# Delta-rule products issued back to back, two ticks ahead of a head's scores, nine idle matmuls for fourteen, and the norm's x loaded later

## The chip, the cores and the metric

One core of a Trainium2 chip. The metric is the device time of one execution in microseconds (us), the median of several runs.

## The reference

One layer with a mixer of three branches and an MLP, on 512 tokens of width 1024, in float32. `rms_norm` scales each token; `proj = h @ w_in` feeds all branches: the gated delta rule (4 heads of 128, in chunks; `step` is one of them), causal stick-breaking attention (8 heads of 64) and a short convolution.

```python
    h = rms_norm(x, norm_mix_pre[l])
    proj = h @ w_in[l]
...
    y_a = gdn_branch(gdn_qkv, gdn_gate, gdn_a, gdn_b, conv_qkv_w[l], gdn_a_log[l],
                     gdn_dt_bias[l], gdn_norm_w[l])
    y_b = stick_breaking_branch(sb_qkv)
    y_c = short_conv_branch(sc_x, sc_b, sc_c, conv_sc_w[l])
...
    merged = (gates[:, :, 0] * (y_a @ w_branch[l, 0]) + gates[:, :, 1] * (y_b @ w_branch[l, 1])
              + gates[:, :, 2] * (y_c @ w_branch[l, 2]))
    x = x + rms_norm(merged @ w_out[l], norm_mix_post[l])
    h = rms_norm(x, norm_ffn_pre[l])
    x = x + rms_norm(jnp.square(jax.nn.relu(h @ w_ff1[l])) @ w_ff2[l], norm_ffn_post[l])

...
def step(state, inp):
    q_c, k_c, u_c, w_c, a_c, gl_c = inp
    v_new = u_c - jnp.einsum("bhcd,bhde->bhce", w_c, state)
    o_c = (jnp.einsum("bhcd,bhde->bhce", q_c, state)
           + jnp.einsum("bhcs,bhse->bhce", a_c, v_new))
    state = state * gl_c[..., None, None] + jnp.einsum("bhcd,bhce->bhde", k_c, v_new)
    return state, o_c
```

## The kernel before, in words

Everything is one program on one core. A float32 product is made of three matmuls on a high and a low part of each operand; a weight is split by a cast on ScalarE (L143) and a subtraction on VectorE (L144) into a tile `hl`, of which there are three buffers. Loads of weights are issued by SyncE, in the order of the program's priorities.

*The start.* L245 and L246 issue `WN` idle matmuls on zeros (`warm`). Then, for each of eight blocks k of the width, xT (`xk`) and the value weights (`raw`) are loaded, x is scaled and split into `xh` and `xl` (L263, L264), and four banks `psv` take the value product, 96 matmuls. The table `XT` says at which k the pieces of `xtok` (x by tokens) are loaded; their squares (ScalarE, L270) are summed to the norm's factor: POOL makes `rstd`, VectorE the diagonal `dg`, PE the matmul `rb` that spreads it over the partitions, ScalarE copies it (L297). With `rb`, VectorE scales `xk` (L301), which is split into `hh` and `hl`; `vv` is the scaled value product, half of it by ScalarE (L308) and half by VectorE (L309). The first two projections (`conv` with NX = 2) use `xh`, `xl` and are scaled afterwards (`cv`, L419), the later ones use `hh`, `hl`. `decay()` sums `psab` over 16 matmuls on `hh` and `hl`, copies it (`abT`, L349), and turns it by four small matmuls into `psa`.

*The middle.* The projections (`proj`, 24 matmuls each) are PE's steady work. The branches are generators in four lanes. `proj` calls `tick()` after k = 2, 5 and 7, so a tick is nine or six matmuls of a projection; at a tick each lane runs its live generator on if the count of its last `yield` is used up. The order of the work is so written out by hand: by the yields' counts (`SBY`, `CY` and others) and by the table `YD`, which adds to single yields. Within it, a scheduler orders each engine's instructions by priority and data.

- `sb_head(h)`: the scores `z` (8 matmuls), then ScalarE and VectorE make the weights (Abs, Exp, Ln, Relu, a scan, a difference, a last Exp), and, `SBY[0]` = 7 ticks later with the offsets of `YD`, ten transposes `at`, which are split into `ah` and `al`. The lane has width 1, so the next head's scores follow when the generator ends. `sb_out` multiplies by `vv` into `pav`, `SBY[1]` ticks later.
- `gdn_chain(h)`: for each of four chunks the products pc, p2, p3, p4 and p5, `CY` ticks apart. Into the bank p5 go the state's product (`ktok`, left half) and the output's product (`AQ`, right half). Tiles that differ in a number alone are shown as one name in the profile, so p2 to p5 all read `p`; `ct` is the chain's scratch. `pa`, `PM`, `pb` and `T64` belong to the inverse before it (`gdn_inverse`).

Later come the branch products, the output projection and the MLP, up to 903 us; nothing of the change lies there.

Of the kernel before, what the change touches and what calls it, by code (L numbers as in the profile page):

```python
# [18 lines left out]
NB = T // P  # L19
# [16 lines left out]
    "mats2": {0: 11, 1: 3},  # L36
    "pair0": {0: 2},
    "pair2": {0: -2, 5: 1, 28: -2, 30: -1},
    "sb0": {0: 3},
    "sb1": {0: 4},  # L40
    "sb2": {0: 3},
    "sb3": {0: 4},
    "sb5": {0: 2},
    "sb6": {0: 1},
    "sb7": {0: 6},
}
SBY = (7, 10)
NX = 2
PFM = 2
WN = 14  # L50
IY = (2, 8, 4)
HY = (3, 3, 1)
CY = (4, 1)
DY = (3, 3)
MY = (1,)
GY = (1, 1, 4, 2, 1, 1, 1)
XT = ((), (), (0,), (1, 2), (3, 4), (5, 6), (7,), ())
VW_NM, VW_CQ, VW_CS, VW_NF, VW_GN = 0, 8, 56, 68, 76
VW = 77

# [2 lines left out]
def trunk_kernel(ctx, tc, keys, xT, xtok, wst, wab, cst, vec, alog, dtb, wpost, wffn, wfpost, out):  # L63
# [12 lines left out]
    def nm(s):  # L76
        cnt[0] += 1
        return f"{s}_{cnt[0]}"

    def g2(s, dt=F32, shape=(P, 512)):  # L80
        return gp.tile(list(shape), dt, tag="g2", name=nm(s))

    def bank(s="c"):
        return pp.tile([P, 512], F32, tag="c", bufs=5, name=nm(s))
# [93 lines left out]
    def mm(o, l, r, start=True, stop=True, more=False):  # L178
        return nc.tensor.matmul(o, l, r, start=start, stop=stop, skip_group_check=more)  # L179
# [6 lines left out]
    def split(hi, lo, src):  # L186
        nc.scalar.copy(hi, src)  # L187
        nc.vector.tensor_tensor(lo, src, rf(hi), ALU.subtract)  # L188
# [56 lines left out]
    pw = bank("warm")  # L245
    for _ in range(WN):  # L246
        mm(pw, wr[:, 0:128], wr)
# [6 lines left out]
    for k in range(KT):  # L254
        with early():
# [9 lines left out]
            split(wv[k][:, 0, :], wv[k][:, 1, :], raw)  # L265
            for j in XT[k]:
                b, hf = j // 2, j % 2
# [140 lines left out]
    qk, vT, gT, ktok, vs, AD, M1, M2, AQ, sqs, wD, ya = ({} for _ in range(12))  # L408
# [142 lines left out]
    def gdn_chain(h):  # L551
        S = None
        ot = vs[h]
        so = sm.tile([P, NB], F32, name=nm("so"))

        Sh = g2("S", F32, (P, NB, P))
        for n in range(NB):
            ct = g2("ct", F32, (P, 4, P))
            bs = slice(n * P, n * P + P)
            oq = None  # L560
            if n == 0:
                R = vs[h][:, 0, :]
            else:
                pc = bank("pc")
                mm(pc[:, 0:128], qk[h][0][:, bs], S)
                mm(pc[:, 128:256], qk[h][1][:, bs], S)
                R = ct[:, 0, :]
                nc.vector.scalar_tensor_tensor(R, pc[:, 0:128], neG[:, n, h:h + 1], vs[h][:, n, :],
                                               ALU.mult, ALU.add)
                oq = ct[:, 1, :]  # L570
                nc.scalar.mul(oq, pc[:, 128:256], eG[:, n, h:h + 1])
                yield CY[h // 2]
            p2 = bank("p2")
            mm(p2[:, 0:128], T64[h][:, n, :], R)
            z0 = ct[:, 2, :]
            nc.vector.tensor_copy(z0, p2[:, 0:128])
            yield CY[h // 2]
            p3 = bank("p3")
            mm(p3[:, 0:128], M2[h][:, n, :], z0)
            Y = ct[:, 3, :]  # L580
            nc.vector.tensor_copy(Y, p3[:, 0:128])
            yield CY[h // 2]
            p4 = bank("p4")
            mm(p4[:, 0:128], T64[h][:, n, :], Y)
            z = ct[:, 2, :]
            nc.vector.tensor_tensor(z, z0, p4[:, 0:128], ALU.subtract)
            if n < NB - 1:
                Xc = ct[:, 0, :]
                nc.vector.tensor_scalar(Xc, z, wD[h][:, n:n + 1], None, ALU.mult)
            yield CY[h // 2]  # L590
            p5 = bank("p5")
            if n < NB - 1:
                mm(p5[:, 0:128], ktok[h][:, n, :], Xc)
                Sn = Sh[:, n, :]
                if n == 0:
                    nc.vector.tensor_copy(Sn, p5[:, 0:128])
                else:
                    nc.vector.scalar_tensor_tensor(Sn, S, gl[:, n, h:h + 1], p5[:, 0:128], ALU.mult, ALU.add)
                S = Sn
            mm(p5[:, 128:256], AQ[h][:, n, :], z)  # L600
            if n == 0:
                nc.vector.tensor_copy(ot[:, n, :], p5[:, 128:256])
            else:
                nc.vector.tensor_tensor(ot[:, n, :], oq, p5[:, 128:256], ALU.add)
            jk = ct[:, 3, :]
            nc.scalar.activation(jk, ot[:, n, :], AF.Square, accum_out=so[:, n:n + 1])
            yield CY[h // 2]
        f = sm.tile([P, NB], F32, tag="f", bufs=2, name=nm("f"))
        c1 = EPS * P * P
        nc.vector.tensor_scalar(f, sqs[h][:, 1, :], c1, c1 * EPS, ALU.mult, ALU.add)  # L610
        nc.vector.tensor_tensor(f, f, so, ALU.add)
        nc.gpsimd.tensor_tensor(f, f, half[:, 0:1].to_broadcast([P, NB]), ALU.pow)
        nc.vector.tensor_tensor(ot, ot, f.unsqueeze(2).to_broadcast([P, NB, P]), ALU.mult)
        yield GY[6]
        po = bank("po")
        for n in range(NB):
            nc.tensor.transpose(po[:, n * P:n * P + P], ot[:, n, :], ident)
        y = g2("y")
        nc.vector.tensor_tensor(y, gT[h], po, ALU.mult)
        ya[h] = (g2("ya", F32R), g2("ya", F32R))  # L620
        split(ya[h][0], ya[h][1], y)
# [38 lines left out]
    def sb_head(h):  # L660
        pz = [bank("z") for _ in range(3)]
        for j in range(3):
            for b, c0 in SEG[j]:
                n, bs = 128 * b + 128, slice(b * P, b * P + P)
                mm(pz[j][:, c0:c0 + n], Qh[h][:, bs], Kt[h][:, :n], True, False)
                mm(pz[j][:, c0:c0 + n], Ql[h][:, bs], Kt[h][:, :n], False, True)
        w, z, c = ([g2(s) for _ in range(3)] for s in ("w", "z", "c"))

        for j in range(3):
            nc.scalar.copy(z[j][:, :N[j]], pz[j][:, :N[j]])  # L670
            c0, m = DIAG[j]
            keep_before(z[j][:, c0:c0 + 128 * m], m)
        for j in range(3):
            n = N[j]
            nc.scalar.activation(w[j][:, :n], z[j][:, :n], AF.Abs)
            (act(w[j][:, :n], w[j][:, :n], AF.Exp, scale=-1.0))
            (act(w[j][:, :n], w[j][:, :n], AF.Ln, bias=1.0))
            nc.scalar.activation(c[j][:, :n], z[j][:, :n], AF.Relu)
            for b, c0 in SEG[j]:
                ks = slice(c0, c0 + 128 * b + 128)  # L680
                back = c[j][:, ks][:, ::-1]
                nc.vector.tensor_tensor_scan(back, back, w[j][:, ks][:, ::-1], 0.0, ALU.add, ALU.add)  # L682
            nc.vector.tensor_tensor(z[j][:, :n], z[j][:, :n], c[j][:, :n], ALU.subtract)  # L683
            (act(z[j][:, :n], z[j][:, :n], AF.Exp))
        yield SBY[0]
        pt = [bank("at") for _ in range(3)]
        K0 = (((0, 0),), ((1, 0), (3, 384)), ((2, 0),))
        where = {b: (j, c0) for j in range(3) for b, c0 in SEG[j]}
        a = {}
        for j in range(3):  # L690
            for sb, c0 in K0[j]:
                for b in range(sb, NB):
                    o = c0 + (b - sb) * P
                    i, q0 = where[b]
                    nc.tensor.transpose(pt[j][:, o:o + P], z[i][:, q0 + sb * P:q0 + sb * P + P], ident)
            n = N[j]
            hi, lo = g2("ah", F32R), g2("al", F32R)
            split(hi[:, :n], lo[:, :n], pt[j][:, :n])
            for sb, c0 in K0[j]:
                m = 512 - sb * P  # L700
                a[sb] = (hi[:, c0:c0 + m], lo[:, c0:c0 + m])
        avl.add(f"av{h}", sb_out(h, a))

    def sb_out(h, a):
        i, e = h // 2, h % 2
        vv = [VV[b, h // 4][:, h % 4].rearrange("p j c -> p (j c)") for b in range(NB)]
        yield SBY[1]
        pav = bank("pav")
        for j in range(2):
            for sb in range(NB):  # L710
                mm(pav[:, sb * P:], vv[sb], a[sb][j], j == 0 and sb == 0, j == 1 and sb == NB - 1)
        if e == 0:
            y32[i] = g2("y32")
        tl = g2("tl")
        nc.scalar.copy(tl[0:64, :], pav[64:128, :])
        nc.vector.tensor_tensor(y32[i][64 * e:64 * e + 64, :], pav[0:64, :], tl[0:64, :], ALU.add)
        if e == 1:
            yb[i] = (g2("yb", F32R), g2("yb", F32R))
            split(yb[i][0], yb[i][1], y32[i])
# [399 lines left out]
    for tb in product(S, lambda u: W[u], lambda u: (S1[u], block(1, 0)(u)), False, 2):  # L1119
# [8 lines left out]
        z, c0 = tb  # L1128
# [97 lines left out]
```

## Time and profile before

| | us |
|---|---|
| median of 3 runs | 904.35 (902.25, 904.35, 904.47) |
| the profiled execution | 905.1 |
| its span | 903.4 |
| mean granted TensorE clock | 0.996 |

The profile is of one execution: the span runs from its first to its last instruction, and the device time beside it is 1.7 us longer. A row of the timeline has an instruction's start, its duration, and in brackets how long its engine sat idle before it and what ended that.

### The profile page before, as it was taken

To read this page: it belongs to the slowest core of one execution; us is meant where nothing else is said; L and a number is where in the kernel's file an instruction comes from. 1 tells how busy PE (TensorE), PEld (TensorE's weight loads), DVE (VectorE), ACT (ScalarE), POOL (GpSimd) and SP (SyncE) were. 2 spreads that over 40 slices of the span, in tenths; PEclk is the share of its full clock that TensorE was granted. 3 is DMA by queue.
4 is the path that set the end of the run, shared out by engine and by line. 5 is a ranking of instruction groups with operands and counts; after the bars stand their busy time and mean duration, and the time that the engine had idled before them with its cause. 6 is when DMAs were issued, how large, how long until landed. Compare 5 with 4: busy or idle time off the path is not lost.

```text
span 903.4 us, 11761 instructions
## 1 busy us (share of the span) xinstructions
PE 885.4 (98%) x4224; PEld 736.7 (82%) x4224; DVE 589.0 (65%) x1026; ACT 452.1 (50%) x825; POOL 105.8 (12%) x165
## 2 busy tenths in 40 slices
PE   9999999999999999999999999999999999999996
PEld 7788888877788888888888878988888888888885
DVE  4885678987777659655565546533334459878886
ACT  6556875657787732233344333322223237566562
POOL 1003221010112120200000111011111000000120
PEclk9999999999999999999999999999999999999998
DMA  9322223222113144524243552299999339566692
GB/s 313 125 86 82 70 79 118 73 103 71 68 38 106 50 127 121 162 90 117 70 152 126 173 191 94 98 288 288 284 286 269 122 111 373 187 194 203 190 267 103
DMA packets 41626, 136.97 MB, mean 152 GB/s; under 512 B 5456, under 2 KB 5456, under 8 KB 41184
## 3 DMA queue, kind: packets, MB, share of 16 engines
q1 hardware_dynamic: 34032, 111.24, 35.2%
q0 software_dynamic: 7248, 24.68, 13.0%
q8 instruction: 33, 0.54, 0.2%
q10 hardware_dynamic: 288, 0.30, 0.1%
q14 instruction: 25, 0.20, 0.1%
HBM read 131.48 MB, written 29.88 MB: 179 GB/s over the span
## 4 chain that ended last, share of the span: by engine, by line
PE 83%; DVE 10%; issue 3%; ACT 3%; DMA 1%; POOL 0%; DVEq 0%; POOLq 0%; SPq 0%; ACTq 0%
PE mm L179 51%; PE Q L179 5%; PE R L179 5%; PE po L179 5%; PE S L179 5%; PE psv L179 2%; PE V L179 2%; DVE hl L144 2%; DVE c L682 2%; PE p L179 2%; DVE z L683 1%; DVE XX L513 1%; PE pg L179 1%; DVE XX L507 1%; PE warm L179 1%
## 5 line engine op out<-in xcount | busy, mean ns | idle before, releaser
L179 PE MATMUL mm<-hh,hl 128*128 128x512 f32 x928 | 306.0, 397 | 0.9 <-ACT ct L729 0.9
L143 ACT CAST hl<-raw 128x1024 fp32r<-128x1024 f32 x116 | 111.6, 962 | 217.7 <-PE mm L179 189.0
L144 DVE TENSOR_TENSOR hl<-raw,hl 128x1024 fp32r<-128x1024 f32 x116 | 129.9, 1120 | 138.1 <-ACT hl L143 137.8
L179 PEld LDWEIGHTS mm<-hh,hl 128*128 128x128 f32 x928 | 174.1, 188 | 35.7 <-ACT ct L729 1.3
L179 PE MATMUL mm<-hl,hl 128*128 128x512 f32 x464 | 181.1, 390 | 0.0
L179 PE MATMUL mm<-h2h,hl 128*128 128x512 f32 (+1 forms) x528 | 155.0, 377 | 0.4 <-ACT h2h L187 0.2
L179 PEld LDWEIGHTS mm<-h2h,hl 128*128 128x128 f32 x528 | 97.2, 188 | 18.8 <-ACT h2h L187 0.8
L179 PEld LDWEIGHTS mm<-hl,hl 128*128 128x128 f32 x464 | 87.5, 189 | 16.0
L179 PE MATMUL mm<-h2l,hl 128*128 128x512 f32 (+1 forms) x264 | 99.5, 377 | 0.1
L997 DVE TENSOR_TENSOR hl<-ch,hl 128x1024 fp32r<-128x1024 f32 x53 | 64.6, 1223 | 6.2 <-ACT hl L996 6.1
L179 PEld LDWEIGHTS mm<-h2l,hl 128*128 128x128 f32 x264 | 49.7, 188 | 9.4 <-DVE h2l L188 0.3
L996 ACT CAST hl<-ch 128x1024 fp32r<-128x1024 f32 x53 | 55.3, 1046 | 0.0
L179 PE MATMUL po<-wo,mg 128*128 128x512 f32 x192 | 45.2, 391 | 0.0
L179 PEld LDWEIGHTS po<-wo,mg 128*128 128x128 f32 x192 | 35.8, 188 | 7.9 <-ACT mg L187 0.3
L179 PE MATMUL Q<-hl,ahi 128*128 128x512 f32 x128 | 39.7, 391 | 0.0
L179 PE MATMUL R<-hl,ahi 128*128 128x512 f32 x128 | 39.4, 389 | 0.0
L168 POOL DMA_DIRECT2D S<-wst x24 | 20.0, 832 | 151.9 <-DMA S<-wst 115.4
L179 PE MATMUL S<-hl,ahi 128*128 128x512 f32 x120 | 37.0, 389 | 0.0
L682 DVE TENSOR_TENSOR_SCAN c<-c,w 128x512 f32<-128x512 f32 (+3 forms) x32 | 25.5, 815 | 15.1 <-ACT w L106 15.0
L187 ACT CAST ahi<-aT 128x512 fp32r<-128x512 f32 x32 | 19.8, 622 | 28.7 <-PE Q L179 12.1
L179 PEld LDWEIGHTS Q<-hl,ahi 128*128 128x128 f32 x128 | 24.0, 188 | 5.7 <-ACT hl L996 0.4
L947 DVE TENSOR_TENSOR aT<-r,mm 128x256 f32<-128x256 f32 x62 | 23.1, 413 | 7.7 <-ACT r L942 7.7
(297 smaller groups left out, 1448.7 us busy)
## 6 DMA issues: line engine op xcount, KB each, us to landing
raw<-wst SPq DMA_DIRECT2D x92, 512.0 KB, 3.3
ch<-S SPq DMA_DIRECT2D x32, 512.0 KB, 4.3
raw<-wst SPq DMA_DIRECT2D x48, 256.0 KB, 3.2
S<-wst POOLq DMA_DIRECT2D x24, 512.0 KB, 8.7
ch<-wst SPq DMA_DIRECT2D x21, 512.0 KB, 5.2
S<-wst SPq DMA_DIRECT2D x16, 512.0 KB, 8.6
S<-S SPq DMA_DIRECT2D x8, 512.0 KB, 8.7
ch<-wst POOLq DMA_DIRECT2D x8, 512.0 KB, 8.7
```

What stands on the lines that cost most here:

```text
L143: nc.scalar.copy(hl[:, 0, :], raw)
L144: nc.vector.tensor_tensor(hl[:, 1, :], raw, rf(hl[:, 0, :]), ALU.subtract)
L168: nc.gpsimd.dma_start(t, wsrc(1024, *key), accum_op=ALU.add, max_dma_last_dim=4096)
L179: return nc.tensor.matmul(o, l, r, start=start, stop=stop, skip_group_check=more)
L187: nc.scalar.copy(hi, src)
L507: nc.vector.tensor_tensor(tmp[:, :, :w], X[:, :, j].unsqueeze(2).to_broadcast([P, 8, w]), L[:, j, j + 1:].unsqueeze(1).to_broadcast([P, 8, ...
L513: nc.vector.tensor_tensor(X[:, :, j + 1:], X[:, :, j + 1:], tmp[:, :, :w], ALU.subtract)
L682: nc.vector.tensor_tensor_scan(back, back, w[j][:, ks][:, ::-1], 0.0, ALU.add, ALU.add)
L683: nc.vector.tensor_tensor(z[j][:, :n], z[j][:, :n], c[j][:, :n], ALU.subtract)
L947: x = nc.vector.tensor_tensor(aT[i][u][:, f % 2, :], r[:, c], ps[:, c], ALU.mult)
L996: after[0] = nc.scalar.copy(hl[0][:, c], r)
L997: after[1] = nc.vector.tensor_tensor(hl[1][:, c], r, rf(hl[0][:, c]), ALU.subtract)
```

## The change

`gdn_chain` issues the product on `AQ` directly behind the one on `ktok`, ahead of VectorE's read of the state. `sb_head` yields two ticks more (`SBY[2]`) behind its transposes, and the offsets of the heads in `YD` are smaller. `WN` goes from 14 to 9. `XT` loads all of xtok at k = 4 to 7.

```diff
-    "sb0": {0: 3},
-    "sb1": {0: 4},
-    "sb2": {0: 3},
-    "sb3": {0: 4},
-    "sb5": {0: 2},
-    "sb6": {0: 1},
-    "sb7": {0: 6},
+    "sb0": {0: 1},
+    "sb1": {0: 2},
+    "sb2": {0: 2},
+    "sb3": {0: 3},
+    "sb4": {0: -2},
+    "sb5": {0: 0},
+    "sb6": {0: -1},
+    "sb7": {0: 5, 1: -2},
 }
-SBY = (7, 10)
+SBY = (7, 10, 2)
-WN = 14
+WN = 9
-XT = ((), (), (0,), (1, 2), (3, 4), (5, 6), (7,), ())
+XT = ((), (), (), (), (0, 1), (2, 3), (4, 5), (6, 7))
@@ gdn_chain
             if n < NB - 1:
                 mm(p5[:, 0:128], ktok[h][:, n, :], Xc)
+            mm(p5[:, 128:256], AQ[h][:, n, :], z)
+            if n < NB - 1:
                 Sn = Sh[:, n, :]
                 if n == 0:
                     nc.vector.tensor_copy(Sn, p5[:, 0:128])
                 else:
                     nc.vector.scalar_tensor_tensor(Sn, S, gl[:, n, h:h + 1], p5[:, 0:128], ALU.mult, ALU.add)
                 S = Sn
-            mm(p5[:, 128:256], AQ[h][:, n, :], z)
@@ sb_head
         avl.add(f"av{h}", sb_out(h, a))
+        yield SBY[2]
```

On PE, where psab ends and psa is issued (`mm_523` of before and `mm_518` of the change are the third projection, 24 matmuls, `hl_519` and `hl_514` its weights). Before:

```order
L179 MATMUL psab_442<-hl,wabs 16x512
L179 MATMUL mm_487<-xh_140,hl_483 128x512
L179 MATMUL mm_523<-hh,hl_519 128x512
...
L179 MATMUL mm_523<-hl,hl_519 128x512
L179 MATMUL mm_523<-hh,hl_519 128x512
L179 MATMUL psa_587<-cs,abT_459 128x8 x4
```

and in the change:

```order
L180 MATMUL psab_437<-hl,wabs 16x512
L180 MATMUL mm_518<-hh,hl_514 128x512 x2
L180 MATMUL mm_518<-hl,hl_514 128x512
L180 MATMUL mm_518<-hh,hl_514 128x512 x2
L180 MATMUL mm_518<-hl,hl_514 128x512
L180 MATMUL mm_518<-hh,hl_514 128x512
L180 MATMUL psa_582<-cs,abT_454 128x8 x4
```

Between the last psab and psa stood 25 projection matmuls, and seven stand there now. The matmul rb has moved the other way: it followed the last of psv directly, and now 15 matmuls of the first projection stand ahead of it.

On ScalarE, at the same place of the program (`hl_624` and `hl_619` are the fifth projection's weights, `hl_660` and `hl_655` the sixth's). Before:

```order
L143 CAST hl_624<-raw_623 128x1024
L308 ACTIVATE vv_385<-psv_238,rstd 128x4x64
L308 ACTIVATE vv_388<-psv_239,rstd 128x4x64
L308 ACTIVATE vv_391<-psv_239,rstd 128x4x64
L308 ACTIVATE vv_394<-psv_240,rstd 128x4x64
L308 ACTIVATE vv_397<-psv_240,rstd 128x4x64
L349 COPY abT_459<-psab_442 16x512
L143 CAST hl_660<-raw_659 128x1024
```

and in the change:

```order
L309 ACTIVATE vv_380<-psv_233,rstd 128x4x64
L309 ACTIVATE vv_383<-psv_234,rstd 128x4x64
L144 CAST hl_655<-raw_654 128x1024
L309 ACTIVATE vv_386<-psv_234,rstd 128x4x64
L309 ACTIVATE vv_389<-psv_235,rstd 128x4x64
L309 ACTIVATE vv_392<-psv_235,rstd 128x4x64
L350 COPY abT_454<-psab_437 16x512
```

The sixth conversion, which stood behind abT, stands ahead of the last three vv and of abT.

On PE, at the last step of the first chunk of the heads 0 and 1 of the delta rule (`p_429` and `p_430` are their banks p5, `mm_2420` and `mm_2415` a projection, `at` the transposes of the sixth attention head). Before:

```order
L179 MATMUL p_429_2430<-ct_2158,ktok_869 128x128
L179 MATMUL p_430_2436<-ct_2164,ktok_1090 128x128
L179 MATMUL mm_2420<-hh,hl_2416 128x512
...
L179 MATMUL mm_2420<-hh,hl_2416 128x512
L179 MATMUL p_429_2430<-ct_2158,AQ_1020 128x128
L179 MATMUL p_430_2436<-ct_2164,AQ_1267 128x128
L695 MATMUL at_2457<-cs,z_2265 128x128
```

and in the change:

```order
L180 MATMUL p_429_2425<-ct_2153,ktok_864 128x128
L180 MATMUL p_429_2425<-ct_2153,AQ_1015 128x128
L180 MATMUL p_430_2431<-ct_2159,ktok_1110 128x128
L180 MATMUL p_430_2431<-ct_2159,AQ_1262 128x128
L180 MATMUL mm_2415<-hh,hl_2411 128x512
L180 MATMUL mm_2415<-hl,hl_2411 128x512
```

The AQ products stood 15 projection matmuls behind the ktok products, directly ahead of the transposes; now each stands behind its ktok product, and nine projection matmuls lie between them and the transposes.

## Rows read from the trace of the kernel before

**Rows 1.** The page, part 1: busy time, share of the span, instructions of each engine.
```profile
PE 885.4 (98%) x4224; PEld 736.7 (82%) x4224; DVE 589.0 (65%) x1026; ACT 452.1 (50%) x825; POOL 105.8 (12%) x165
```
**Rows 2.** Waits of PE: who waited, for whom; us in total, times, longest.
```profile
PE warm L179 <- DVE wr L244: 2.0, 1, 2.0
PE p L179 <- DVE S L596: 1.8, 1, 1.8
PE z L179 <- DVE al L188: 1.0, 1, 1.0
PE mm L179 <- ACT ct L729: 0.9, 1, 0.9
PE p L179 <- DVE ct L581: 0.8, 1, 0.8
...
PE z L179 <- DVE K L648: 0.7, 1, 0.7
PE pb L179 <- ACT PM L538: 0.5, 1, 0.5
PE p L179 <- DVE S L598: 0.3, 1, 0.3
...
PE p L179 <- DVE ct L568: 0.2, 1, 0.2
```
**Rows 3.** Windows: length, busy time of PE, PEld, DVE, ACT, POOL, PEclk, DMA share, GB/s.
```profile
250.20:253.55 3.35, 3.35 (x15) 3.16 (x14) 3.05 (x6) 2.05 (x8) 0.00 (x0) 0.50 0.19 45
...
176.00:178.00 2.00, 1.73 (x9) 1.48 (x10) 1.97 (x8) 2.00 (x6) 1.03 (x3) 1.00 0.00 0
```
**Rows 4.** Timeline of PE around the wait for S.
```profile
249.01 0.71 PE L179 MATMUL p<-ct,AQ 128*128 128x128 f32 x4 [1.83 <-DVE S L596]
249.56 1.72 PE L695 MATMUL at<-cs,z 128*128 128x128 f32 x10
```
**Rows 5.** Timeline of PE at the start: first idle matmul, first psv, rb.
```profile
1.98 6.19 PE L179 MATMUL warm<-wr 128*128 128x512 f32 x14 [1.98 <-DVE wr L244]
8.00 0.63 PE L179 MATMUL psv<-hl,xh 128*128 128x512 f32 x2
...
29.80 1.02 PE L179 MATMUL rb<-dg,cs 128*128 128x512 f32 x2
```
**Rows 6.** Timeline of ScalarE: the weights of the first two blocks.
```profile
4.92 0.60 ACT L187 CAST hl<-raw 128x512 fp32r<-128x512 f32 x1
...
9.10 0.62 ACT L187 CAST hl<-raw 128x512 fp32r<-128x512 f32 x1
```
**Rows 7.** Timeline of PE: last matmuls of the second and third projection, psa.
```profile
45.15 0.39 PE L179 MATMUL mm<-xh,hl 128*128 128x512 f32 x1
...
50.59 0.39 PE L179 MATMUL mm<-hh,hl 128*128 128x512 f32 x1
51.16 1.05 PE L179 MATMUL psa<-cs,abT 16*128 16x8 f32 x8 [0.17 <-ACT abT L349]
```
**Rows 8.** Timeline of ScalarE ahead of psa.
```profile
45.62 1.05 ACT L143 CAST hl<-raw 128x1024 fp32r<-128x1024 f32 x1 [1.47 <-issue]
46.58 0.83 ACT L308 ACTIVATE vv<-psv,rstd 128x256 fp32r<-128x256 f32 x2
...
50.54 0.56 ACT L349 COPY abT<-psab 16x512 f32<-16x512 f32 x1
```
**Rows 9.** Timeline of VectorE ahead of psa.
```profile
46.71 1.22 DVE L144 TENSOR_TENSOR hl<-raw,hl 128x1024 fp32r<-128x1024 f32 x1 [1.57 <-ACT hl L143]
47.85 0.87 DVE L309 SCALAR_TENSOR_TENSOR vv<-psv,rstd,vv 128x256 fp32r<-128x256 f32 x2
```
**Rows 10.** Timeline: first scores (PE) and last exp (ScalarE), fifth and eighth head.
```profile
206.10 0.47 PE L179 MATMUL z<-K,Qh 128*128 128x512 f32 x1 [0.73 <-DVE K L648]
...
217.88 0.42 ACT L106 ACTIVATE z<-z 128x256 f32<-128x256 f32 x1 [0.96 <-DVE z L683]
...
276.16 0.39 PE L179 MATMUL z<-K,Qh 128*128 128x512 f32 x1
...
287.72 0.42 ACT L106 ACTIVATE z<-z 128x256 f32<-128x256 f32 x1 [0.70 <-DVE z L683]
```

## The prediction

> **What bounds the kernel now.** I read the page's busy times first: TensorE's matmuls are busy for 98% of the span, VectorE for 65%, ScalarE for 50% [rows 1]. So only about 18 us exist in which PE does nothing, and the change leaves the number of useful matmuls as it is; whatever it wins or loses must be a PE wait, or a stretch in which PE's clock is low. The second view is therefore the list of PE's waits [rows 2]: 2.0 us before the first idle matmul, and eight short waits that belong to the branches that share the middle of the program: 1.8 on S, 1.0 on al, 0.9 on ct (L729), 0.8 on ct (L581), 0.7 on K, 0.5 on PM, 0.3 on S again and 0.2 on ct (L568), together 6.2 us, all of them between 176 and 289 us. The third is the windows view: after the longest of those waits the granted clock is 0.50 for 3.35 us, which is 1.2 GHz instead of 2.4; around the 1.0 us wait on al it stays at 1.00 [rows 3]. The fourth is the timeline at that place: the output products of the delta rule, `p<-ct,AQ`, sat 1.83 us behind VectorE's read of S [rows 4].
>
> **The start, idle matmuls.** Fourteen idle matmuls run from 1.98 to 8.00, 0.43 us apiece, and the 96 real ones after them take (29.80 - 8.00)/96 = 0.227 us apiece with no gap, up to the matmul rb [rows 5]. That is the low and the high level of the clock. With nine, the first real matmul can start at 1.98 + 9 x 0.43 = 5.85; its operands are there, since ScalarE's half of the first weights is done at 4.92 + 0.60 = 5.52 [rows 6]. PE has been at work for equally long at 8.0, so I let the clock rise there as before: five real matmuls run at 0.43 in place of five idle ones, and 5 x 0.227 = 1.13 us are won behind them. The other seven of the first input block end at 8.00 + 7 x 0.227 = 9.59; the second block's weights are ready at 9.10 + 0.62 = 9.72 [rows 6], a gap of 0.15. Term: **-1.0** (0 if the clock rises later by as much, -1.1 at best). Bringing xtok later gives these matmuls nothing by itself: they ran without a gap already.
>
> **The start, xtok.** What the later xtok does is to move its consumers. In the order of PE, rb stands 15 matmuls deeper, behind the value product rather than directly after it; its successors are pushed together, and psa, which had 25 projection matmuls between itself and the last psab, has seven. ScalarE's order changes with it: one more weight conversion (the one two behind hl_519, now called hl_655) stands ahead of three vv and of abT, where it used to stand behind abT. A conversion writes one of three weight buffers, and this one's is the buffer that the third projection reads until its last matmul. So ScalarE cannot pass before that projection ends, and psa, the very next thing on PE, needs abT from behind it. The same pattern one projection earlier gives the price: the last matmul of the second projection starts at 45.15 [rows 7], and then the conversion starts at 45.62 and ends near 46.58, the next two vv take 0.83 [rows 8], VectorE's half starts at 46.71 and is followed by two vv from 47.85, 0.87 long [rows 9]. Put in terms of the last matmul's start: conversion +0.47 to +1.43, two vv to +2.26, VectorE's half to +2.70, its two vv to +3.57, the last vv on ScalarE to +4.0, abT (0.56 [rows 8]) to +4.56, psa at **+4.6**. Before, psa started 51.16 - 50.59 = 0.57 behind the last matmul, 0.17 of it waiting [rows 7]. Term: **+4.0**, a PE wait of about 4.2 us that no row of before has. Least: +2.5, if ScalarE's vv do not wait for VectorE's; most: +5.0, if the conversion's own buffer is late too.
>
> **The clock after that wait.** No row shows a wait of 4.2 us inside the program. The nearest are the 1.83 us wait, after which 3.35 us ran at 0.50 and so lost 1.67 us [rows 3, 4], and the launch, where PE worked for 8.00 - 1.98 = 6.0 us at the low level, 3.0 us lost [rows 5]. The waits of up to 1.0 lost nothing [rows 2, 3]. I take the middle of the two losses, **+2.3**; 0 and +3.0 are the ends.
>
> **The middle, removed.** The two products of a step are issued back to back, so the output product no longer sits behind the read of S: that removes the 1.83 and the 0.3 [rows 2, 4]. The two ticks ahead of each next head's scores put 15 to 18 projection matmuls (3.4 to 4.1 us at 0.227) between the transposes and the scores, so the scores' wait for al, which is the copy of those transposes, goes, and so does that for K (0.7). The other four (0.9, 0.8, 0.5, 0.2) stand at places that the new offsets move as well, and in the new order their producers stand further ahead. I take all eight, 6.2 us, and the 1.67 us of low clock behind the longest: **-7.9**. The least is -4.6: the two on S, the one on al and the clock alone, with 0.2 to spare.
>
> What reads S now waits for two products rather than one. Two output products take 249.56 - 249.01 = 0.55 us [rows 4], so S comes 0.28 us later in each of twelve steps. In the order the next user of S stands six to nine matmuls away (1.4 to 2.0 us), so nothing of it shows; 12 x 0.28 = 3.3 us is the far end. Here the Trainium skill speaks against the change: PSUM — Partial Sum Buffer, section "PSUM bank collisions raise a hardware error", says that two engines are kept apart by bank and quadrant, and that another address in the same bank still collides. By that rule reading S must wait for the second product, as I have assumed, and the sum would be at most 3.3 us higher if nothing covered it; the trace agrees in so far as the output product, in the other half of the bank, waited 1.83 us for the read.
>
> **The middle, new waits.** The scores come later, the transposes mostly do not, so the chain from scores to transposes has less room. For the eighth head it takes 287.72 + 0.42 - 276.16 = 12.0 us from the first scores to the last exp, for the fifth 217.88 + 0.42 - 206.10 = 12.2 [rows 10]. In the new order the eighth head has 8 score matmuls (1.2 us), 21 of projections (4.8), 8 of pav (1.2), 9 small products (9 x 0.28 = 2.5) and 2 of psd (0.5) in between: 10.2 us, so its transposes wait about 1.7. The fifth head has 38 of projections (8.6), the scores (1.2), 8 products of pb (1.8) and 2 of p2 (0.6): 12.2, which is just enough; I take 0.5. A further 0.3 is for the output of the fifth head, whose copy stands close behind VectorE's other work. Term: **+2.5** (0 to +7).
>
> **The sum** is -1.0 + 4.0 + 2.3 - 7.9 + 2.5 = **-0.1 us**. The profiled execution took 905.1 us with a span of 903.4; the median of the three runs is 904.35. So I forecast **904.2 us**. About 0.3%, 2.7 us, is what a measurement of this kernel can tell from no change.
>
> **Rival 1, the waits simply go.** The wait at psa comes, but PE's clock does not fall behind it, and half of the new waits in the middle stay hidden: -1.0 + 4.0 - 7.9 + 1.2 = -3.7, 900.6 us. For it: the waits of up to 1.0 us left the clock at 1.00 [rows 3]. Against it: 1.83 us did not, and 4.2 is longer. If the wait at psa did not come either, it would be 896.6; the order speaks against that.
>
> **Rival 2, slower: the transposes wait.** In the middle the two ticks shift the waits from the scores to the transposes. If the fifth, sixth, seventh and eighth heads each wait 1.2 to 1.7 us there (the chain is 12 us or longer, and VectorE was busy for most of the stretch), that is 5.5 us in place of 2.5, and one of them is long enough to drop the clock again (1.67 [rows 3]): -0.1 + 3.0 + 1.7 = +4.6, **909.0 us**. It decides from the point where the new waits with their clock pass 5.3 us, as -0.1 + 2.8 is then the bound. Against it: the sixth and seventh heads have 17 and 13.5 us of work in between.
>
> **Rival 3, the idle matmuls matter.** With nine of them the clock could rise later than 8.0: each further microsecond at the low level costs 0.5. With 3 us more the first term is +0.5 in place of -1.0, and the time 905.7; that is inside the forecast's own range. The Trainium skill (TensorE: Matmul & The Clock Gate, Part 1) adds that the number of cold matmuls at the start varies from run to run of one kernel; a single trace can't show this.
>
> **How the numbers follow.** The forecast's case, within 2.7 us of the time before, gets 0.46: two terms of about 6.3 and 7.9 stand against each other, and each is uncertain by 2. Rival 1, with all that is faster by over 0.3%, gets 0.35: the removed waits are rows, the new ones are argued. Rival 2, with all that is slower by over 0.3%, gets 0.19. The range goes from 898.8 to 907.8: below lies the case without any wait at psa, above a rival 2 in full. The forecast's own case reaches from 901.6 to 907.1.
>
> **What would show it.** In the profile after: the first real matmul at about 5.9 and rb near 32; PE idle for about 4.2 us ahead of psa, released by abT, at 54; a granted clock of 0.50 in the microseconds behind it; no `p<-ct,AQ` waiting for S, no z waiting for al; the eighth head's transposes waiting for z. If PE passes psa with under 2 us of idle time, or at full clock, the kernel is faster than I say; if the list of waits shows more than 5 us on transposes, slower.

## The result, and the profile after

The changed kernel takes 910.53 us (median of 6 runs, 910.0 to 911.49) against 904.41 for the kernel before: 6.1 us more, a ratio of 1.0073 with a 95% interval of 1.006 to 1.0086. The forecast was 904.2, with a range to 907.8; the result lies above the range.

The page's first part of the changed kernel, to be read beside [rows 1]:

```profile
PE 886.3 (97%) x4219; PEld 737.4 (81%) x4219; DVE 590.1 (65%) x1026; ACT 452.9 (50%) x825; POOL 106.1 (12%) x165
```

PE is busy 0.9 us more while the span is 6.3 us longer (909.7 against 903.4): most of the loss is idle time, and some is work at half clock, which counts as busy. The waits of PE, which answer to [rows 2] (engine and line that waited, the one waited for, us in total, times, longest):

```profile
PE psa L180 <- ACT abT L350: 4.2, 1, 4.2
...
PE p L180 <- DVE ct L569: 1.7, 1, 1.7
PE p L180 <- DVE ct L590: 1.6, 1, 1.6
PE pa L180 <- DVE TN L531: 1.4, 1, 1.4
PE mm L180 <- DVE cv L736: 1.4, 1, 1.4
PE p L180 <- DVE T L546: 0.7, 1, 0.7
PE po L180 <- ACT mg L188: 0.7, 1, 0.7
PE pc L180 <- DVE S L601: 0.7, 1, 0.7
```

All eight waits of [rows 2] that the prediction adds up are gone. In their place stand one of 4.2 us at psa and six in the middle, 1.7 + 1.6 + 1.4 + 1.4 + 0.7 + 0.7 = 7.5 us; the one on mg lies outside it. None of the six is a transpose `at`. (`cv` at L736 belongs to the short convolution, `TN` and `T` to the delta rule's inverse.)

The start, by the timelines of PE, ScalarE and VectorE around psa (start, duration, instruction, idle time before it and what ended it), to be read beside [rows 7 to 9]:

```profile
49.53 0.39 PE L180 MATMUL mm<-hh,hl 128*128 128x512 f32 x1
54.11 1.73 PE L180 MATMUL psa<-cs,abT 16*128 16x8 f32 x8 [4.19 <-ACT abT L350]
```
```profile
50.00 1.04 ACT L144 CAST hl<-raw 128x1024 fp32r<-128x1024 f32 x1 [0.74 <-ACT vv L309]
50.95 0.83 ACT L309 ACTIVATE vv<-psv,rstd 128x256 fp32r<-128x256 f32 x2
53.12 0.47 ACT L309 ACTIVATE vv<-psv,rstd 128x256 fp32r<-128x256 f32 x1 [1.34 <-DVE vv L310]
53.50 0.56 ACT L350 COPY abT<-psab 16x512 f32<-16x512 f32 x1
```
```profile
51.08 1.23 DVE L145 TENSOR_TENSOR hl<-raw,hl 128x1024 fp32r<-128x1024 f32 x1 [1.28 <-ACT hl L144]
52.22 0.87 DVE L310 SCALAR_TENSOR_TENSOR vv<-psv,rstd,vv 128x256 fp32r<-128x256 f32 x2
```

The chain is the forecast one: the third projection's last matmul at 49.53, the conversion 0.47 later, two vv, VectorE's half with two vv, the last vv, abT, and psa 4.58 after that matmul. The windows behind it (length, busy time of PE, PEld, DVE, ACT, POOL, granted clock, DMA share, GB/s):

```profile
54.20:61.20 7.00, 7.00 (x21) 5.81 (x22) 6.59 (x13) 2.68 (x7) 0.00 (x0) 0.51 0.10 40
...
293.00:294.00 1.00, 0.78 (x3) 0.78 (x4) 1.00 (x4) 0.20 (x1) 0.00 (x0) 0.61 0.39 156
294.00:295.00 1.00, 1.00 (x5) 0.90 (x4) 1.00 (x2) 1.00 (x4) 0.00 (x0) 0.50 0.03 8
295.00:296.00 1.00, 1.00 (x4) 0.71 (x4) 1.00 (x4) 0.83 (x3) 0.00 (x0) 0.50 0.00 0
296.00:297.00 1.00, 1.00 (x5) 0.81 (x4) 0.90 (x3) 0.95 (x2) 0.00 (x0) 0.68 0.00 0
```

The clock is at its lower level, 1.2 GHz, for 7 us behind psa, and again, for most of 293 to 297, behind the waits on ct and S; there 0.39 + 0.50 + 0.50 + 0.32 = 1.7 us are lost.

Where the time went, by the start of the same instruction in both profiles:

| | before | after | later by |
|---|---|---|---|
| psa | 51.16 | 54.11 | 2.95 |
| first psg | 72.67 | 78.78 | 6.11 |
| first matmul on yc | 310.56 | 316.88 | 6.32 |
| first matmul on h2h | 564.83 | 571.13 | 6.30 |
| first Q | 742.44 | 748.98 | 6.54 |

So the net loss is all made by 79 us; the middle, from which 5.4 us were to come back, gave nothing.

### The profile page after: what moved, and what is told of

It reads as the page before. It is cut to its first block, busy times and chain, and to the rows that moved or that the text cites. A ratio compares the mean times of both kernels' runs of the same rounds, so it can differ in the third digit from the quotient of the medians.

```text
span 909.7 us, 11758 instructions
## 1 busy us (share of the span) xinstructions
PE 886.3 (97%) x4219; PEld 737.4 (81%) x4219; DVE 590.1 (65%) x1026; ACT 452.9 (50%) x825; POOL 106.1 (12%) x165
## 4 chain that ended last, share of the span: by engine, by line
PE 83%; DVE 8%; issue 3%; ACT 3%; DMA 2%; POOL 0%; SPq 0%; POOLq 0%; DVEq 0%; ACTq 0%
PE mm L180 54%; PE Q L180 5%; PE R L180 5%; PE S L180 4%; PE po L180 3%; PE V L180 2%; PE psv L180 2%; DMA raw<-wst 2%; DVE hl L145 2%; PE p L180 2%; DVE c L684 1%; ACT hl L144 1%; DVE XX L514 1%; PE pg L180 1%; DVE XX L508 1%
## 5 line engine op out<-in xcount | busy, mean ns | idle before, releaser
L180 PEld LDWEIGHTS mm<-hh,hl 128*128 128x128 f32 x928 | 176.1, 190 | 37.6 <-DVE cv L736 1.8
```

## The experiments

Eleven kernels; a ratio is to the kernel before, measured beside it (medians of 904.17 to 904.85). Theory A, first formed from the table above: the start loses 6 us at psa and in the clock behind it, and the middle's old and new waits cancel. The rivals stand with each run.

### One part of the change at a time

**Early xtok.** The changed kernel with one line undone:

```diff
-XT = ((), (), (), (), (0, 1), (2, 3), (4, 5), (6, 7))
+XT = ((), (), (0,), (1, 2), (3, 4), (5, 6), (7,), ())
```

> The changed kernel with the table of the xtok loads of the kernel before (nine idle matmuls, both products back to back and the two ticks stay). Theory A (the whole loss sits at psa and in the clock behind it; the middle's removed and new waits cancel): the wait at psa falls from 4.2 to under 0.4 us, the granted clock stays at 1.00 between 54 and 62 us, psa starts near 50.2, and the time is about 904.4 - 1.0 + 0.1 = 903.5, 7 us under the changed kernel. Theory B (the middle's new waits are the loss): the time stays over 907.

Measured: 904.50, ratio 1.0002 (0.9991 to 1.0013). The clock behind psa stays at 1.00 and the wait there is what it was before the change:

```profile
49.92 1.05 PE L180 MATMUL psa<-cs,abT 16*128 16x8 f32 x8 [0.18 <-ACT abT L350]
```

The late xtok is the whole net loss, within a microsecond of theory A; the other three edits together are neutral.

**The conversion behind abT.** The changed kernel, xtok late, with one rule of order added:

```diff
-            nc.scalar.copy(hl[:, 0, :], raw)
+            cast = nc.scalar.copy(hl[:, 0, :], raw)
+            held.append(cast)
+            if len(held) == 6:
+                dep(cast, ab[0])
...
-        nc.scalar.copy(abT[:16, :], psab[:16, :])
+        ab.append(nc.scalar.copy(abT[:16, :], psab[:16, :]))
```

> The changed kernel, xtok late as it is, but the sixth weight conversion on ScalarE is held behind abT; the order on PE is word for word that of the changed kernel. Theory A (the conversion, which waits for the third projection's end, is what makes psa late): the wait at psa falls from 4.2 to under 0.5 us, no low clock behind it, time about 903.5. Rival (the late factor of the norm itself is the cause, by rb, hh and psab): psa or the next matmul still waits over 2 us, time over 906.

Measured: 910.04, ratio 1.0055 (1.0038 to 1.0072). The wait falls by 1.9 us only, and the clock still falls behind it. Timeline of PE and of ScalarE, and the window behind psa:

```profile
52.92 1.87 PE L184 MATMUL psa<-cs,abT 16*128 16x8 f32 x8 [2.31 <-ACT abT L354]
```
```profile
51.94 0.47 ACT L313 ACTIVATE vv<-psv,rstd 128x256 fp32r<-128x256 f32 x1 [0.58 <-DVE vv L314]
52.31 0.56 ACT L354 COPY abT<-psab 16x512 f32<-16x512 f32 x1
```
```profile
54.73:59.60 4.87, 4.87 (x13) 3.81 (x13) 4.76 (x8) 2.25 (x6) 0.00 (x0) 0.50 0.34 108
```

So the rival holds as well: without the conversion, abT still ends 2.3 us too late, behind vv that stand later than before the change. The conversion is 1.9 of the 4.2 us; the rest goes with the late xtok too, since early xtok removes both, and I put it down to the late rb and its successors. The trace bears this out: VectorE scales the last blocks with rb at 45.28 and starts its first vv at 46.60, where before it was 41.35 and 42.67. It was not tried by itself. This run's profile also shows a wait of 1.4 us between the first and the second input block (0.2 in the changed kernel's), which is part of why its gain is small.

**The products alone.** The kernel before with the edit in `gdn_chain`.

```diff
                 mm(p5[:, 0:128], ktok[h][:, n, :], Xc)
+            mm(p5[:, 128:256], AQ[h][:, n, :], z)
+            if n < NB - 1:
                 Sn = Sh[:, n, :]
...
-            mm(p5[:, 128:256], AQ[h][:, n, :], z)
```

> The kernel before with one edit: the product on AQ directly behind the one on ktok. Theory A (a wait in a queue, taken away): the waits of 1.8 and 0.3 us on S and the 3.35 us at half clock go, nothing takes their place, time 904.4 - 3.8 = 900.6. Rival (reading S a product later makes the chain late elsewhere): new waits of p or pc on S or ct of 2 us or more, time 903 to 905.

Measured: 901.64, ratio 0.9969 (0.9958 to 0.998). The two waits on S and the half clock at 250 are gone. Small waits come up: 0.5 on the chain's output ahead of pav, 0.2 ahead of a transpose, and 0.9 in place of 0.2 on ct (L568); the gain is 3.1 us where 3.8 was expected. The read of S does wait for the second product: six of the twelve reads start 0.03 to 0.04 us behind its end, the other six later. One of the six, on PE and on VectorE:

```profile
398.59 0.39 PE L179 MATMUL p<-ct,AQ 128*128 128x128 f32 x2
```
```profile
399.01 0.29 DVE L598 COPY S<-p 128x128 f32<-128x128 f32 x1 [0.34 <-PE p L179]
```

No wait of PE on S is left in this run.

**The ticks alone.** The kernel before with `SBY[2]` and the offsets of the change.

```diff
-SBY = (7, 10)
+SBY = (7, 10, 2)
...
+        yield SBY[2]
```

> The kernel before with the two ticks and the head offsets of the change alone. Theory A (the ticks bring the delta rule's chain and the attention heads on VectorE into each other's way: they remove some 4 us of waits and make about 9): slower, 906 to 909, with the waits on cv, TN, T, ct near 1 to 2 us each. Rival (each of the two edits of the middle is neutral alone): 904 to 905.

Measured: 905.84, ratio 1.0015 (1.0005 to 1.0025): slower by 1.1 us, less than expected. The longest waits of PE are the new ones of the changed kernel, and one on S:

```profile
PE p L180 <- DVE ct L590: 1.9, 1, 1.9
PE p L180 <- DVE ct L569: 1.7, 1, 1.7
PE pa L180 <- DVE TN L531: 1.4, 1, 1.4
PE mm L180 <- DVE cv L735: 1.4, 1, 1.4
PE p L180 <- DVE S L597: 1.0, 1, 1.0
```

The ticks bring the new waits by themselves. They also shorten the wait on S from 1.8 to 1.0, and no half clock follows it; in this profile one follows the 1.9 us on ct instead and costs another 1.7:

```profile
287.20:290.70 3.50, 3.42 (x12) 2.46 (x12) 3.21 (x8) 2.08 (x6) 0.00 (x0) 0.52 0.31 117
```

So the two edits remove in part the same thing: alone they are worth -3.1 and +1.1, together, with nine idle matmuls, -0.2.

**Nine idle matmuls.** The kernel of the products alone with `WN` = 9.

```diff
-WN = 14
+WN = 9
```

> The kernel before with both products back to back and nine idle matmuls, xtok and head offsets as before. Theory A (nine idle matmuls win 1.0 us with xtok early): 901.6 - 1.0 = 900.6, the first real matmul near 6, psa near 50.0. Rival (the clock rises later, or a gap for data opens): within 0.5 of 901.6 or above it.

Measured: 901.46, ratio 0.9966 (0.9953 to 0.9979); 0.2 us under the run with 14, which is within the uncertainty. In its profile psa starts at 49.85 against 50.62, so 0.8 us are won there. Over all profiles with xtok early, psa starts at 49.4 to 50.1 in the six with nine idle matmuls and at 50.6 to 51.2 in the three with 14, which is 1.05 between the means. In this run PE waits 0.7 us for the second block's weights:

```profile
9.32 1.42 PE L179 MATMUL psv<-hl,xh 128*128 128x512 f32 x5 [0.73 <-ACT hl L187]
```

That wait is between nothing and 1.4 us in the profiles of the runs with nine: PE now has to wait there for data in most of them.

**The start alone.** The kernel before with nine idle matmuls and the late xtok.

```diff
-WN = 14
+WN = 9
-XT = ((), (), (0,), (1, 2), (3, 4), (5, 6), (7,), ())
+XT = ((), (), (), (), (0, 1), (2, 3), (4, 5), (6, 7))
```

> The kernel before with nine idle matmuls and the late xtok alone. Theory A (the start makes the whole loss): a wait at psa of about 4.2 us and a half clock of 6 to 7 us behind it, time 904.7 + 6.1 = 910.8. Rival (what is lost at the start is caught up in the middle, or the middle of the kernel before adds to it): under 908 or over 913.

Measured: 911.01, ratio 1.0065 (1.0052 to 1.0079): 6.2 us, as theory A had it, with a wait of 4.19 us at psa.

### Why the middle gave nothing

The new waits had not been placed there. Going back from the waits on cv and TN: VectorE was idle for 5.75 us ahead of the fourth head's first scan, and then had that head, a short convolution and the inverse's copies all at once. Timelines of ScalarE, POOL and VectorE of the changed kernel; the fourth head's scores were issued on PE at 182.00 to 183.14.

```profile
186.93 1.06 ACT L144 CAST hl<-raw 128x1024 fp32r<-128x1024 f32 x1 [5.71 <-PE mm L180]
...
188.36 1.35 ACT L672 COPY z<-z 128x512 f32<-128x512 f32 x3
192.83 0.63 ACT L677 ACTIVATE w<-z 128x512 f32<-128x512 f32 x1 [3.12 <-POOL z L653]
```
```profile
188.99 0.57 POOL L517 DMA_DIRECT2D scr<-XX  x1 [27.37 <-DVE XX L514]
191.58 0.90 POOL L520 DMA_DIRECT2D tc<-scr  x1 [2.02 <-DMA scr<-XX]
192.49 0.90 POOL L653 TENSOR_SCALAR_AFFINE_SELECT z<-z 128x128 f32<-128x128 f32 x3
```
```profile
195.58 1.23 DVE L684 TENSOR_TENSOR_SCAN c<-c,w 128x512 f32<-128x512 f32 x1 [5.75 <-ACT w L107]
```

Two things hold the fourth head: a weight conversion on ScalarE that waits 5.71 us for a projection's end (the same pattern as at psa), and the causal mask on POOL (`keep_before`, L653), which stands behind the two transfers of the delta rule's inverse; the first of these waits for VectorE's inverse, the second for the first. In the kernel before the mask stood ahead of both; POOL's timeline there:

```profile
176.88 1.24 POOL L651 TENSOR_SCALAR_AFFINE_SELECT z<-z 128x128 f32<-128x128 f32 x3 [21.21 <-ACT z L670]
185.66 0.57 POOL L516 DMA_DIRECT2D scr<-XX  x1 [7.54 <-DVE XX L513]
```

**Theory C, the conversion.** Early xtok, and the 26th conversion held behind the copies of the fourth head's scores.

```diff
-            nc.scalar.copy(hl[:, 0, :], raw)
+            cast = nc.scalar.copy(hl[:, 0, :], raw)
+            held.append(cast)
+            if len(held) == 26:
+                dep(cast, zc[11])
...
-            nc.scalar.copy(z[j][:, :N[j]], pz[j][:, :N[j]])
+            zc.append(nc.scalar.copy(z[j][:, :N[j]], pz[j][:, :N[j]]))
```

> The run with early xtok (both products, two ticks, nine idle matmuls), and the 26th weight conversion on ScalarE, which waited 5.7 us for a projection to end, held behind the copies of the fourth head's scores; the scheduler then also moves some matmuls of PE between 196 and 210 us. Theory C (this conversion made the fourth head 5 us late, and VectorE's work piled up behind it): VectorE's idle time of 6.1 us ahead of the fourth head's first scan goes, the waits of PE on cv (1.7), TN (1.4) and T (0.7) fall to under 1 us together, time about 904.5 - 3.3 = 901.2. Rival (VectorE is simply full there by the two ticks): the three waits stay within 1 us of 3.9, time 904 to 905.

Measured: 906.19, ratio 1.0022 (1.0011 to 1.0034): theory C falls as the sole cause. The copies come 5.6 us earlier, at 175.44, but ScalarE then waits 4.96 us for the mask, w starts at 185.74 where it had started at 185.87, and PE waits 2.7 us for TN.

**Theory D, the mask.** The run before, and the inverse issues its two transfers later in the program, so that the mask comes first on POOL.

```diff
+        if h0 == 0:
+            yield 3
         nc.gpsimd.dma_start(scr2.rearrange("x n b (q m) c -> (x n b q) (m c)", q=4), X.rearrange("p m i -> p (m i)"))
-        yield IY[0]
+        yield IY[0] if h0 else 1
...
-        yield IY[1]
+        yield IY[1] if h0 else 6
```

> The run with the scores first, and in addition the inverse issues its two transfers three and two ticks later in the program, so that on POOL's queue the mask of the fourth head stands ahead of them instead of behind (its transposes TT stay at their tick). Theory D (the fourth head's mask sat on POOL behind the two transfers of the inverse, which wait for VectorE and for each other; so ScalarE and VectorE sat idle 5 to 6 us and then had everything at once): ScalarE starts on w within 2 us of the copies, near 177; VectorE's idle time of 6 us ahead of the fourth head's first scan is gone; the waits of PE on cv, TN and T together fall from 3.9 to about 1 us; time 904.5 - 2.9 = 901.6. Rival (VectorE is full there anyway): the waits stay at 3 us or more, time 903.5 to 906.

Measured: 900.31, ratio 0.9962 (0.9947 to 0.9976); the fastest kernel of the study. POOL's timeline, and the waits of PE in the middle that are left, beside one of 0.4 on K:

```profile
175.49 0.29 POOL L659 TENSOR_SCALAR_AFFINE_SELECT z<-z 128x128 f32<-128x128 f32 x1 [21.68 <-ACT z L678]
...
181.40 0.57 POOL L523 DMA_DIRECT2D scr<-XX  x1 [3.86 <-DVE XX L518]
```
```profile
PE p L184 <- DVE ct L575: 1.7, 1, 1.7
PE pc L184 <- DVE S L607: 1.5, 1, 1.5
PE p L184 <- DVE T L552: 1.3, 1, 1.3
PE p L184 <- DVE ct L596: 0.7, 1, 0.7
```

ScalarE starts on w at 176.10, VectorE on the scan at 181.02 with no idle time of 6 us, and the waits on cv and TN are gone; the one on T stays at the 1.3 that it had with the scores first (0.7 in the changed kernel). With the conversion already moved, the mask's place is worth 906.19 - 900.31 = 5.9 us by the medians, 5.2 when each is taken against the kernel before beside it. Much of that is clock: in the profile of the scores first the clock is low from 201.7 to 208.5 around the 2.7 us wait on TN, and again from 290 to 293.6; in this profile it does not fall while PE has work.

```profile
201.70:208.50 6.80, 6.11 (x19) 5.24 (x20) 5.72 (x11) 3.40 (x7) 0.00 (x0) 0.50 0.22 77
```

**One tick.** Early xtok, and the fourth head's scores one tick earlier, its transposes where they were.

```diff
-    "sb2": {0: 2},
-    "sb3": {0: 3},
+    "sb2": {0: 2, 1: -1},
+    "sb3": {0: 4},
```

> The run with early xtok (both products, two ticks, nine idle matmuls) with the fourth head's scores one tick earlier and its transposes at the old tick (second offset of sb2 -1, first of sb3 4): on POOL the mask then stands ahead of the inverse's transfers, and on ScalarE the copies of the scores ahead of the 26th conversion, with no other rule added. Theory D: as above, the waits on cv, TN and T go, time 904.5 - 3.9 = 900.6. Rival (the two ticks cost in themselves): 903.5 or more.

Measured: 903.45, ratio 1.0000 (0.999 to 1.001): no different from the kernel before, and 0.5 to 1.1 us under early xtok, not 3.9. The mask does stand first (POOL starts it at 174.51), and cv and TN no longer wait; but ScalarE now finishes more of the head before the copy that a projection needs, and PE waits 2.5 us for that (`mm` on ct, L732). Moving by ticks moves everything behind as well.

**Both losses in the changed kernel.** The change itself, xtok late, with the order of theory D's run (its edits are those of that run).

> The changed kernel itself, xtok late, with the order of the run before on POOL and ScalarE (the fourth head's mask ahead of the inverse's transfers, its copies ahead of the 26th conversion). Theory D with theory A (two separate losses, one at psa, one at the fourth head's mask): the wait at psa stays 4.2 us with 7 us of low clock behind it, the waits on cv and TN go, time 910.5 - 4.2 = 906.3. Rival (the late start shifts the engines against each other, so that the mask's place no longer matters): 909 or more.

Measured: 907.82, ratio 1.0036 (1.0022 to 1.0049): 2.7 us under the changed kernel's 910.53. psa waits 4.19 as before, cv and TN wait no longer, T waits 1.3. That is 2.2 us of waits less. The two losses are separate; the gain is smaller than forecast by 1.5.

**The last four heads.** Theory D's run, the two ticks for the first four heads alone.

```diff
-        yield SBY[2]
+        if h < 4:
+            yield SBY[2]
...
-    "sb4": {0: -2},
-    "sb5": {0: 0},
-    "sb6": {0: -1},
-    "sb7": {0: 5, 1: -2},
+    "sb5": {0: 2},
+    "sb6": {0: 1},
+    "sb7": {0: 6},
```

> The run with the mask ahead of the transfers, with the two ticks for the first four heads alone and the offsets of the last four as in the kernel before; the delta rule of heads 2 and 3 then starts a few ticks earlier in the program. Theory E (the waits on ct and S between 255 and 290 us, 4.0 us in that run, come from the two ticks of the last four heads): they fall to about the 1.9 us of the run with the two products alone, time 900.3 - 2.0 = 898.3. Rival (they come from the products issued back to back): they stay near 4 us, time 900 to 901.

Measured: 901.12, ratio 0.9969 (0.9955 to 0.9982). The waits between 255 and 290 us stay: 1.7 on ct, 1.3 on ct, 0.8 ahead of pc, and two that end with w, 1.1. Theory E falls. Since this edit also moves the delta rule of the last two heads in the program, it does not show what these waits come from; that stays open. The trace of the changed kernel shows what stands ahead of the small steps on VectorE. The step on ct (L569) at 271.48 comes behind the scans and differences of the seventh head, with VectorE busy without a break from 265.49; the other (L590) behind a weight's subtraction:

```profile
269.45 1.26 DVE L684 TENSOR_TENSOR_SCAN c<-c,w 128x384 f32<-128x384 f32 x2
...
271.48 0.34 DVE L569 SCALAR_TENSOR_TENSOR ct<-pc,neG,vs 128x128 f32<-128x128 f32 x1
...
288.72 2.09 DVE L145 TENSOR_TENSOR hl<-raw,hl 128x1024 fp32r<-128x1024 f32 x1 [0.39 <-ACT hl L144]
290.73 1.07 DVE L590 TENSOR_SCALAR ct<-ct,wD 128x128 f32<-128x128 f32 x1
```

No run moved these steps alone, so this is read and not tested.

## Why the prediction was wrong, point by point

- *Idle matmuls, -1.0.* Right where it was forecast: behind the same work the third projection ends 1.06 earlier (49.53 against 50.59 [rows 7]), although the medians with xtok early differ by 0.2 only, which the measurement can't tell from 1. That the size fits so well is luck in part: the clock rises at another time in each profile (the first five real matmuls end between 6.80 and 8.12, in the changed kernel at 7.38), and the gap for the second block, put at 0.15, is 0 to 1.4. The first real matmul starts at 5.99 (5.85 forecast).
- *xtok, +4.0.* Right, in the place and the size: 2.95 + 1.06 = 4.0, with 4.19 us idle and psa at 54.11 where 54 was written. Its account goes by the conversion alone; the run with abT first shows that this is 1.9 us, and that a wait of 2.3 would be left without it.
- *The clock behind it, +2.3.* Low by 0.9: from psa to psg the changed kernel falls back by 6.11 - 2.95 = 3.2 us. The upper end, 3.0, was nearer. The clock is low for 6.8 us, twice as long as behind the 1.83 us wait, and the term had been put between the two lengths.
- *The middle, removed, -7.9.* All eight waits are gone, and the half clock at 250.
- *The middle, new waits, +2.5.* **The step that failed.** It asked only whether the chain from scores to transposes fits between the two on PE, with that chain's length taken from the kernel before. In the changed kernel no transpose waits. Six other waits of 7.5 us stand there, with a half clock behind the last two (1.7): +9.2 in place of +2.5. Two of the six, on cv and TN (2.8 us), come of the fourth head: its chain became 5 to 6 us late on POOL's and ScalarE's queues, which the prediction did not read past psa, and both waits go when the conversion is held back and the mask stands first. The other four, on T, ct twice and S (4.7 us), are still there with the mask first (1.3 + 1.7 + 1.6 + 0.7 in the changed kernel); those on T and ct are there with the ticks alone, too. That VectorE's queue holds them is read from the trace only, and their cause stays open. The half clock behind ct and S is not a fixed part of the loss: it came in three of the five profiles with the same two waits.
- *The sum.* The start was to cost 5.3 and costs -1.06 + 4.0 + 3.2 = 6.1 by 79 us; the middle was to give back 5.4 and gives nothing. By its rows the middle would be -7.9 + 9.2 = +1.3, and by the starts of the same instructions it is +0.2; the other 1.1 us I can't account for. Between the first psg and the first matmul on yc PE idles 1.2 us more than before (237.9 us long with 231.3 busy, now 238.1 with 230.3), as the rows say, but it is busy 1.0 us less.

Rival 2 had nearly the time (909.0) and the kind of loss, new waits in the middle that eat what was won, but not the place: it put them on four transposes. Its sign, more than 5 us of waits on transposes, never showed, so that its time came near is luck. Of the edits, the products win 3.1 us by themselves, the ticks lose 1.1, nine idle matmuls bring psa forward by 1.0 in the profiles without a gain in the time that can be measured, and the late xtok loses 6. That the reading of S after both products would matter was bounded at 3.3 us; the products alone gain 3.1 of 3.8, and as no wait on S is left there, none of the missing 0.7 is seen to come of it. By the rule of the Trainium skill (PSUM — Partial Sum Buffer, section "PSUM bank collisions raise a hardware error") the read must wait for the second product. The trace agrees: six of the twelve reads start within 0.04 us of its end.

## What to carry to other kernels

When an order written by hand shifts by a tick, read the queues of the small engines past every moved step: one instruction that waits (a transfer of an inverse on POOL, a conversion waiting for a buffer on ScalarE) ahead of another chain's short step can cost that chain the whole wait, and the work that it delays then runs together on another engine. A length of a chain taken from the old trace holds only if each queue it passes keeps its order. And a load that is "early enough" for its data can still be late for the scheduler: moving xtok cost 6 us without one transfer being waited for by PE.

## What the runs showed of the hardware

The length of a wait alone does not tell whether PE's clock falls behind it or within it. It fell to 1.2 GHz at waits of 1.83 [rows 3, 4], 1.88 (ticks alone), 1.53 and 2.31 (abT first), 2.74 (scores first) and 4.19 us; it stayed at 1.00 behind 1.75 and 1.72 (early xtok), behind 1.72 and 1.53 (mask first), and behind 2.47 (one tick). The plainest case is one pair of waits, on ct and 1.4 us later on S, which stands at the same place of five kernels:

| | wait on ct, on S | low clock |
|---|---|---|
| the changed kernel | 1.64, 0.66 | 3.4 us |
| scores first | 1.66, 0.66 | 3.4 us |
| one tick | 1.64, 0.66 | 3.4 us |
| early xtok | 1.66, 0.66 | none |
| mask first in the changed kernel | 1.65, 0.66 | none |

In three rows of windows, one tick and early xtok at this pair, and one tick behind its 2.47:

```profile
285.30:288.70 3.40, 3.33 (x10) 2.85 (x11) 3.40 (x9) 2.56 (x6) 0.00 (x0) 0.53 0.12 47
```
```profile
285.00:293.00 8.00, 7.31 (x38) 5.41 (x39) 6.65 (x14) 6.01 (x17) 0.64 (x1) 1.00 0.17 65
```
```profile
187.50:192.50 5.00, 4.99 (x23) 4.18 (x24) 4.68 (x8) 1.98 (x3) 2.79 (x5) 1.00 0.39 131
```

Where it fell, it stayed low for 3.4 us at waits of up to 1.9 us and for 6.8 us at those of 2.31, 2.74 and 4.19; what PE works through of that costs half its length, so 1.7 us or up to 3.4. So a fall behind a wait is a term with two ends, and the length that is forecast for the wait does not choose between them.
